# Single transposes between the wide matmuls of a projection, in a fixed order, in place of blocks of four or eight

## The chip, the cores and the metric

The kernel runs on one core of one Trainium2 chip. The core has five engines that work side by side, each through its own list of instructions: TensorE (PE in the profile; its weight loads are listed as PEld) multiplies matrices into PSUM banks, VectorE (DVE) and ScalarE (ACT) do arithmetic on rows, GpSimd (POOL) does slower arithmetic and issues DMAs, SyncE (SP) issues DMAs. The engines wait for one another by semaphores. The metric is the device time of one execution in microseconds, a median over runs.

## The reference

Two layers work on 2048 latent tokens and 256 context tokens of 1024 numbers each. Layer 0 is latent attention beside gated linear attention; layer 1, around which most of the change lies, is a neighbourhood attention with a gate:

```python
h = rms_norm(x, norm_g[i]) * (1 + scale) + shift          # hc likewise from the context
...
q, k, v, z = jnp.split(jnp.dot(h, w_in), 4, axis=-1)      # od_w_in is 1024 x 4096
q, k = rms_norm(sh(q), q_gain), rms_norm(sh(k), k_gain)   # 16 heads of 64
o = neighborhood_attention(q, k, v, k_ctx, v_ctx, rpb)    # window of 8 x 16 on a grid of 32 x 64, and the context
y = jnp.dot(o.reshape(h.shape[0], h.shape[1], C_WIDTH) * jax.nn.silu(z), w_out)
x = x + gate * y
```

Layer 0 has gates of the same form: a projection z times the sigmoid of itself, multiplied onto the attention's output. All is float32.

## The kernel before, in words

**Tiles.** The 256 context and 2048 latent tokens are 18 tiles of 128 tokens (`NT`, two of them context, `NCT`). A projection of a tile is done in cells: one cell is one tile by one block of 512 output columns. The 1024 inputs are eight steps of 128. A float32 product is three products of reduced parts (high by high, high by low, low by high), so that a cell is 8 x 3 = 24 matmuls of 128 x 128 by 512 columns into one PSUM bank. These are the wide matmuls, lines L129 to L131 in `mm3_steps` (L120 to L122 in `mm3`, which other stages use). Their tile is named `gm`.

**Stages.** One after the other on TensorE, with some overlap: layer 0's latent projections, layer 0's gates and the rest of its projections (`even_rest`), layer 0's attention, its output projection, layer 1's queries, keys and half of a gate (`odd_qk`), layer 1's values and the other gates (`odd_vz`), layer 1's attention and output.

**Where transposes stand.** The matmul contracts over partitions, so what comes out with tokens on partitions must be transposed wherever the next product wants it the other way. A transpose is a matmul against the identity, 128 columns.

- `transposed` (L318 to L332): a tile's normalized x, eight transposes into two PSUM banks `px` (L331), once per tile in `odd_qk` and in layer 0. `modulate` scales and shifts them on ScalarE, splits them into high and low parts on VectorE (tiles `hhi`, `hlo`) and stores the result to H from ScalarE's DMA queue. In the later stages `reload` loads H back and splits it (L357).
- `odd_qk`, cell L1117 to L1141, `fin` L1143 to L1182: a finished cell is squared on ScalarE (`osq`), summed on VectorE and raised to a power on GpSimd (`oss`), scaled on VectorE (`onat`, L1139). A gate cell (j = 6) has a tanh on ScalarE and a product on VectorE instead. The cell goes to a list `pend`; `fin` transposes it four times into one bank `tp` (L1147), splits it (`oqh`, `oql`, `okt`) and stores it: queries and keys on SyncE's queue, keys in a second form and the gates on GpSimd's.
- `odd_vz`, cell L1221 to L1243: the cells j = 6 and 7 of latent tiles are gates: tanh, product (`ovz`, L1199), four transposes (L1239), a copy `ozt`, a store on ScalarE's queue.
- `even_rest`, cell L611 to L636: the same for column block 0, with tiles `u` and `zt`; 18 such cells.

**Score maxima.** In `even_rest` and `odd_vz` a second stream of matmuls runs between the projection's: scores of queries against keys, of which VectorE takes row maxima. In `odd_vz` (L1251 to L1300) they are two 256-column matmuls per pair of query tiles (L1273) and one of up to 480 columns per query tile (L1280) into five banks `mx`; GpSimd builds a table of bias and mask for every head (`mtab`, L1258 and L1259).

**What sets the order.** The code of the kernel is traced once; every instruction has a priority by its place in the trace. A planner, which simulates the engines when the kernel is built, then orders each engine's instructions: of those whose inputs it believes ready it takes the first by priority. `issue_after(a)` binds an instruction to come behind `a` on its engine; the rest is free. `weave` draws wide matmuls (three at a time) and score matmuls alternately at a given ratio and binds the wide ones behind earlier score matmuls. `stream` goes through the cells and prepares the next tile when a tile's last cell is done. `pump` draws splits of the next weights (`split_steps`, tiles `wraw` to `w0h` and so on), which ScalarE and VectorE do.

In `odd_qk` the transposes of a cell come into the trace in the middle of a later cell:

```python
for n, _ in enumerate(steps):
    if n == 5 and pend and (len(pend) > 1 or j == 6):
        fin(*pend.pop(0))
    yield
```

with `n` the step of eight. Everywhere else they come right behind what makes their input, and the planner places them by its own times.

Of the kernel before, what the change touches and what calls it, by code (L numbers as in the profile page):

```python
# [17 lines left out]
P = 128  # L18
D = 1024
KD = D // P  # L20
# [4 lines left out]
NCT = CTX // P  # L25
# [63 lines left out]
class Kern:  # L89
    def __init__(self, tc, nc, ins, scr):  # L90
        self.tc, self.nc, self.i, self.scr = tc, nc, ins, scr
        self.n = 0
        self.ahead, self.calls, self.chain = [], 0, None

# [19 lines left out]
    def mm3(self, out, lhs, rhs, ks, start=True, stop=True):  # L114

        lh, ll = lhs
        rh, rl = rhs
        n = len(ks)
        for j, k in enumerate(ks):
            self.nc.tensor.matmul(out, lh(k), rh(k), start=start and j == 0, stop=False)  # L120
            self.nc.tensor.matmul(out, lh(k), rl(k), start=False, stop=False)
            self.nc.tensor.matmul(out, ll(k), rh(k), start=False, stop=stop and j == n - 1)  # L122

    def mm3_steps(self, out, lhs, rhs, ks):
        lh, ll = lhs
        rh, rl = rhs
        n = len(ks)
        for j, k in enumerate(ks):
            self.nc.tensor.matmul(out, lh(k), rh(k), start=j == 0, stop=False)  # L129
            self.nc.tensor.matmul(out, lh(k), rl(k), start=False, stop=False)  # L130
            yield self.nc.tensor.matmul(out, ll(k), rh(k), start=False, stop=j == n - 1)  # L131
# [46 lines left out]
    def stream(self, cells, hT, cell, prep, done=None):  # L178
# [8 lines left out]
        for n, (t, j) in enumerate(cells):  # L187
            yield from cell(t, j)
# [128 lines left out]

    def transposed(self, t, src, pp, tag, xp=None):  # L318

# [9 lines left out]
        ps = [self.tl(pp, [P, 4, P], tag[0], bufs=tag[1]) for _ in range(2)]  # L329
        for k in range(KD):  # L330
            nc.tensor.transpose(ps[k // 4][:, k % 4, :], x[:, k * P : k * P + P], self.ident[:])  # L331
        return x, ps, hi, lo  # L332
# [267 lines left out]
    def even_rest(self, ws, win, hT):  # L600
        nc = self.nc
        self.zaT = self.scr("zaT", (4, P, T), F32)
        with ExitStack() as es:
# [5 lines left out]
            def cell(t, j):  # L609
# [12 lines left out]
                if j == 0:  # L622
                    pt = self.tl(pp, [P, 4, P], "tp", bufs=1)
                    for b in range(4):
                        nc.tensor.transpose(pt[:, b, :], u[:, b * P : b * P + P], self.ident[:])
                    z = self.tl(sp, [P, 4, P], "zt")
                    self.act(z[:], pt[:])
                    nc.gpsimd.dma_start(self.zaT[:, :, t * P : t * P + P].rearrange("j p t -> p j t"), z[:])
                elif j == 1:
                    nc.gpsimd.dma_start(self.Un[t, :, 1056:], u[:])  # L630
                else:
                    nc.gpsimd.dma_start(self.Un[t, :, (j - 2) * 352 : (j - 1) * 352], u[:, :352])

# [1059 lines left out]
```

## Time and profile before

| | us |
|---|---|
| median of 3 runs | 3750.93 |
| lowest and highest of these | 3749.34 and 3751.32 |
| the profiled execution, span | 3751.7 |
| layer 0, latent projections (0 to 552 of the span): TensorE busy | 510.7 |
| `even_rest` (552 to 1092): TensorE busy | 533.3 |
| layer 0's attention (1092 to 1986): TensorE busy | 880.6 |
| layer 0's output projection (1986 to 2189): TensorE busy | 201.3 |
| `odd_qk` (2189 to 2644): TensorE busy | 436.8 |
| `odd_vz` (2644 to 3118): TensorE busy | 462.2 |
| layer 1's attention and output (3118 to the end): TensorE busy | 562.1 |

The span is the profiled execution's own time, from its first instruction to its last. The stage borders are read from where the lines of TensorE change. How the rows shown below are read: in the first part of the page stand each engine's busy time, its share of the span and its number of instructions. A row of a stretch has start and end, length, the busy times of TensorE, its weight loads, VectorE, ScalarE and GpSimd with their instructions in brackets, then the granted TensorE clock (1 is full speed), the busy share of the DMA engines and GB/s. A row of the timeline has start, duration, engine, line, operation, output and inputs, shape; `x4` means that four instructions stand together in it; a bracket at the end names a wait, its length, and what ended it. A row of waits has who waits, what ended it, the total, the number of times and the longest.

### The profile page before, as it was taken

To read this page: it belongs to the slowest core of one execution; us is meant where nothing else is said; L and a number is where in the kernel's file an instruction comes from. 1 tells how busy PE (TensorE), PEld (TensorE's weight loads), DVE (VectorE), ACT (ScalarE), POOL (GpSimd) and SP (SyncE) were. 2 spreads that over 40 slices of the span, in tenths; PEclk is the share of its full clock that TensorE was granted. 3 is DMA by queue.
4 is the path that set the end of the run, shared out by engine and by line. 5 is a ranking of instruction groups with operands and counts; after the bars stand their busy time and mean duration, and the time that the engine had idled before them with its cause. 6 is when DMAs were issued, how large, how long until landed. Compare 5 with 4: busy or idle time off the path is not lost.

```text
span 3751.7 us, 51747 instructions
## 1 busy us (share of the span) xinstructions
PE 3587.1 (96%) x18404; PEld 2772.4 (74%) x18404; DVE 2375.7 (63%) x4860; ACT 1437.8 (38%) x2741; POOL 1206.8 (32%) x1336
## 2 busy tenths in 40 slices
PE   7999989999999999999999999999899999898889
PEld 6988988888886666656657878887688886555567
DVE  4677656888866666696754344455578774666722
ACT  4445541111125555545552134444222224444400
POOL 1434320010111222212202233333444435776643
PEclk9999999999999999999999999999999999999899
DMA  7455453222252231425515545545544448777464
GB/s 254 138 161 162 130 168 96 80 81 80 77 134 66 75 108 57 117 82 149 143 37 180 162 141 155 148 146 166 178 138 147 127 114 225 188 183 201 140 194 131
DMA packets 364371, 512.18 MB, mean 137 GB/s; under 512 B 25825, under 2 KB 243889, under 8 KB 358210
## 3 DMA queue, kind: packets, MB, share of 16 engines
q1 hardware_dynamic: 322642, 425.49, 39.5%
q0 software_dynamic: 19872, 55.92, 4.9%
q10 hardware_dynamic: 21600, 27.46, 2.1%
q8 instruction: 146, 2.39, 0.3%
q14 instruction: 111, 0.91, 0.1%
HBM read 329.38 MB, written 179.37 MB: 136 GB/s over the span
## 4 chain that ended last, share of the span: by engine, by line
PE 78%; DVE 8%; DMA 6%; POOL 4%; ACT 3%; issue 2%; SPq 0%; POOLq 0%; DVEq 0%; ACTq 0%
PE gm L129 9%; PE gm L130 9%; PE gm L131 9%; PE av L905 7%; PE st L963 4%; PE mx L651 4%; PE st L964 3%; PE st L965 3%; PE pj L129 3%; PE pj L130 3%; PE pj L131 3%; POOL oacc L1409 2%; PE o L1403 1%; DMA wraw<-w_od 1%; PE st L1373 1%
## 5 line engine op out<-in xcount | busy, mean ns | idle before, releaser
L954 DVE TENSOR_TENSOR acc<-acc,apt 128x512 f32<-128x512 f32 x512 | 364.6, 737 | 155.3 <-ACT apt L106 152.3
L106 ACT ACTIVATE apt<-st 128x512 f32<-128x512 f32 (+1 forms) x592 | 343.9, 593 | 282.5 <-PE st L965 245.3
L652 DVE TENSOR_REDUCE mm<-mx 128x1 f32<-128x512 f32 (+1 forms) x656 | 389.2, 629 | 82.1 <-PE mx L651 75.1
L905 PE MATMUL av<-apt,av 128*64 128x512 f32 (+1 forms) x1184 | 286.2, 597 | 0.0
L963 PE MATMUL st<-aq,akh 97*128 97x512 f32 (+1 forms) x592 | 254.0, 429 | 5.8 <-ACT apt L106 3.0
L1409 POOL TENSOR_TENSOR oacc<-oacc,opt 128x576 f32<-128x576 f32 (+6 forms) x192 | 221.4, 1178 | 87.0 <-ACT opt L106 85.3
L651 PE MATMUL mx<-mk,mq 96*128 96x512 f32 (+1 forms) x656 | 236.8, 373 | 6.1 <-DMA mq<-QT 4.7
L964 PE MATMUL st<-aq,akh 96*128 96x512 f32 (+1 forms) x592 | 235.1, 397 | 0.0
L965 PE MATMUL st<-aq,akl 96*128 96x512 f32 (+1 forms) x592 | 234.0, 396 | 0.0
L1286 DVE CUSTOM_DVE_ANT_1 mx<-mx,mtab 128x225 f32<-128x225 f32 (+12 forms) x576 | 183.8, 339 | 61.4 <-PE mx L1280 45.9
L106 ACT ACTIVATE u<-gm 128x352 f32<-128x352 f32 (+1 forms) x140 | 68.5, 497 | 369.8 <-PE gm L131 208.8
L905 PEld LDWEIGHTS av<-apt,av 128*64 128x64 f32 x1184 | 81.6, 137 | 155.3 <-issue 154.1
L1531 DVE TENSOR_TENSOR opt<-st,tab 128x64 f32<-128x64 f32 (+10 forms) x576 | 142.5, 314 | 78.7 <-PE st L1374 50.8
L963 PEld LDWEIGHTS st<-aq,akh 97*128 97x128 f32 x592 | 112.4, 190 | 98.9 <-issue 43.7
L1073 POOL TENSOR_TENSOR px<-py,px 128x512 f32<-128x512 f32 x64 | 86.2, 1348 | 231.5 <-DVE py L1072 220.4
L106 ACT ACTIVATE opt<-opt 128x930 f32<-128x930 f32 (+8 forms) x130 | 104.4, 805 | 138.1 <-DVE opt L1531 129.3
L1373 PE MATMUL st<-q,kt 128*128 128x480 f32 (+5 forms) x256 | 104.3, 409 | 47.2 <-DVE opt L1531 42.5
L651 PEld LDWEIGHTS mx<-mk,mq 96*128 96x128 f32 x656 | 121.7, 189 | 17.7 <-issue 5.1
L106 ACT ACTIVATE prh<-pr 128x1024 fp32r<-128x1024 f32 x32 | 33.9, 1058 | 263.4 <-PE pj L130 235.7
L965 PEld LDWEIGHTS st<-aq,akl 96*128 96x128 f32 x592 | 113.5, 192 | 25.5
L964 PEld LDWEIGHTS st<-aq,akh 96*128 96x128 f32 x592 | 114.1, 193 | 18.0
L106 ACT ACTIVATE x<-px,modB,modA 128x128 f32<-128x128 f32 x272 | 99.1, 468 | 57.9 <-DVE onat L1139 27.6
(513 smaller groups left out, 10054.6 us busy)
## 6 DMA issues: line engine op xcount, KB each, us to landing
q<-Q SPq DMA_DIRECT2D x48, 512.0 KB
H<-x ACTq DMA_DIRECT2D x36, 512.0 KB
adaw<-ada_w SPq DMA_DIRECT2D x64, 256.0 KB
x<-H SPq DMA_DIRECT2D x32, 512.0 KB
pr<-RT SPq DMA_DIRECT2D x32, 512.0 KB
wraw<-w_od SPq DMA_DIRECT2D x64, 256.0 KB
K1t<-okt POOLq DMA_DIRECT2D x32, 512.0 KB, 7.7
kt<-K1t SPq DMA_DIRECT2D x32, 512.0 KB
```

The source lines that it names most:

```text
L106: return self.nc.scalar.activation(out, in_, func, **kw)
L129: self.nc.tensor.matmul(out, lh(k), rh(k), start=j == 0, stop=False)
L130: self.nc.tensor.matmul(out, lh(k), rl(k), start=False, stop=False)
L131: yield self.nc.tensor.matmul(out, ll(k), rh(k), start=False, stop=j == n - 1)
L651: mm = nc.tensor.matmul(ps[:, :w], q[:A_QK, (t % 6) * P : (t % 6) * P + P], k[:A_QK, k0 : k0 + w], start=True, stop=True)
L652: nc.vector.tensor_reduce(out=m[:, t, n : n + 1], in_=ps[:, :w], axis=AX.X, op=ALU.max)
L905: nc.tensor.matmul(O[j, nb][i * 64 : i * 64 + 64, :w], V[j, kt // TT][:, kt % TT, i * 64 : i * 64 + 64], pts[i][:, :w], start=n == 0, stop ...
L954: nc.vector.tensor_tensor(out=acc[i][:, :w], in0=a[:, :w], in1=pts[i][:, :w], op=ALU.add)
L963: nc.tensor.matmul(ps[:, :w], kh[: A_QK + 1, i, kq], qh[: A_QK + 1, :w], start=True, stop=False)
L964: nc.tensor.matmul(ps[:, :w], kh[:A_QK, i, kq], ql[:A_QK, :w], start=False, stop=False)
L965: mm = nc.tensor.matmul(ps[:, :w], kl[:A_QK, i, kq], qh[:A_QK, :w], start=False, stop=True)
L1409: self.psum = nc.gpsimd.tensor_tensor(out=a, in0=a, in1=pts[:, :, a0 - r0 : a1 - r0, :], op=ALU.add)
```

## The change

Transposes of the four places above no longer come in blocks. A new list `narrow` holds tasks; a task is a generator of transposes with a due count and a spacing. Every wide matmul of `mm3` and `mm3_steps` now goes through `mm`, which counts it (`wide`), and, if a task is due, emits that task's next transpose bound behind this wide matmul; the next wide matmul is bound behind the transpose (`hold`). The task is then due again three wide matmuls later. So the order of wide matmuls and transposes is as traced; score matmuls and all other engines stay with the planner.

- A tile's x in `odd_qk`: `prep_task`, due 26 wide matmuls after the tile that frees its buffers has ended; `stream` finishes what is left of it before the tile's first cell.
- A projection in `odd_qk`: queued at step 2 of a later cell, at once due, where it was emitted as a block at step 5. What follows the transposes (`split`) is traced behind the last of them.
- Gates of `odd_vz` and `even_rest`: queued at the end of their cell, due nine wide matmuls later.

Transposes still in the list at the end of a stage are emitted in a block (`finish_tasks`). The numbers of instructions on every engine are the same in both kernels: 16410 on TensorE, 4862 on VectorE, 2705 on ScalarE, 1341 on GpSimd, 1151 on SyncE as built.

```diff
         self.ahead, self.calls, self.chain = [], 0, None
+        self.narrow, self.wide, self.hold = [], 0, None
     def pool(self, es, name, bufs=1, space=None, **kw):
...
         return self.chain
-    def mm3(self, out, lhs, rhs, ks, start=True, stop=True):
-
-        lh, ll = lhs
-        rh, rl = rhs
-        n = len(ks)
-        for j, k in enumerate(ks):
-            self.nc.tensor.matmul(out, lh(k), rh(k), start=start and j == 0, stop=False)
-            self.nc.tensor.matmul(out, lh(k), rl(k), start=False, stop=False)
-            self.nc.tensor.matmul(out, ll(k), rh(k), start=False, stop=stop and j == n - 1)
+    def queue(self, gen, wait=0, every=3):
+        task = [self.wide + wait, every, gen]
+        self.narrow.append(task)
+        return task
+    def finish_tasks(self):
+        while self.narrow:
+            self.finish_task(self.narrow[0])
+    def finish_task(self, task):
+        if task in self.narrow:
+            self.narrow.remove(task)
+        for _ in task[2]:
+            pass
+    def mm(self, out, l, r, start, stop):
+        with self.tc.issue_after(self.hold.ins) if self.hold else ExitStack():
+            mm = self.nc.tensor.matmul(out, l, r, start=start, stop=stop)
+        self.hold = None
+        self.wide += 1
+        for task in self.narrow:
+            if task[0] <= self.wide:
+                with self.tc.issue_after(mm.ins):
+                    self.hold = next(task[2], None)
+                if self.hold is None:
+                    self.narrow.remove(task)
+                task[0] = self.wide + task[1]
+                break
+        return mm
+    def mm3(self, *a):
+        for _ in self.mm3_steps(*a):
+            pass
     def mm3_steps(self, out, lhs, rhs, ks):
...
         for j, k in enumerate(ks):
-            self.nc.tensor.matmul(out, lh(k), rh(k), start=j == 0, stop=False)
-            self.nc.tensor.matmul(out, lh(k), rl(k), start=False, stop=False)
-            yield self.nc.tensor.matmul(out, ll(k), rh(k), start=False, stop=j == n - 1)
+            self.mm(out, lh(k), rh(k), j == 0, False)
+            self.mm(out, lh(k), rl(k), False, False)
+            yield self.mm(out, ll(k), rh(k), False, j == n - 1)
+    def transposes(self, ps, parts, src, done):
+        for n, i in enumerate(parts):
+            t = self.nc.tensor.transpose(ps(i), src(i), self.ident[:])
+            if n == len(parts) - 1:
+                done()
+            yield t
     def weave(self, main, side, ratio, lag, head=0):
...
         for n, (t, j) in enumerate(cells):
+            if len(hT[t]) > 2:
+                self.finish_task(hT[t][2])
+                hT[t] = hT[t][:2]
             yield from cell(t, j)
...
         return self.modulate(l, t, *self.transposed(t, src, pp, tag))
+    def prep_task(self, l, t, src, pp, tag, wait):
+        x, hi, lo = self.scaled(t, src)
+        def steps():
+            ps = []
+            for g in range(2):
+                ps.append(self.tl(pp, [P, 4, P], tag[0], bufs=tag[1]))
+                done = (lambda: self.modulate(l, t, x, ps, hi, lo)) if g else lambda: None
+                yield from self.transposes(lambda k: ps[g][:, k, :], range(4), lambda k: x[:, (g * 4 + k) * P : (g * 4 + k + 1) * P], done)
+        return hi, lo, self.queue(steps(), wait)
     def transposed(self, t, src, pp, tag, xp=None):
+        x, hi, lo = self.scaled(t, src, xp)
+        ps = [self.tl(pp, [P, 4, P], tag[0], bufs=tag[1]) for _ in range(2)]
+        for k in range(KD):
+            self.nc.tensor.transpose(ps[k // 4][:, k % 4, :], x[:, k * P : k * P + P], self.ident[:])
+        return x, ps, hi, lo
+    def scaled(self, t, src, xp=None):
         nc, sp = self.nc, self.prp
...
         nc.vector.tensor_scalar(out=x[:], in0=x[:], scalar1=ss[:, 1:2], scalar2=None, op0=ALU.mult)
-        ps = [self.tl(pp, [P, 4, P], tag[0], bufs=tag[1]) for _ in range(2)]
-        for k in range(KD):
-            nc.tensor.transpose(ps[k // 4][:, k % 4, :], x[:, k * P : k * P + P], self.ident[:])
-        return x, ps, hi, lo
+        return x, hi, lo
     def modulate(self, l, t, x, ps, hi, lo):
...
                 if j == 0:
-                    pt = self.tl(pp, [P, 4, P], "tp", bufs=1)
-                    for b in range(4):
-                        nc.tensor.transpose(pt[:, b, :], u[:, b * P : b * P + P], self.ident[:])
-                    z = self.tl(sp, [P, 4, P], "zt")
-                    self.act(z[:], pt[:])
-                    nc.gpsimd.dma_start(self.zaT[:, :, t * P : t * P + P].rearrange("j p t -> p j t"), z[:])
+                    self.queue(turned(t, u), 9)
                 elif j == 1:
                     nc.gpsimd.dma_start(self.Un[t, :, 1056:], u[:])
                 else:
                     nc.gpsimd.dma_start(self.Un[t, :, (j - 2) * 352 : (j - 1) * 352], u[:, :352])
+            def turned(t, u):
+                pt = self.tl(pp, [P, 4, P], "tp", bufs=1)
+                def store():
+                    z = self.tl(sp, [P, 4, P], "zt")
+                    self.act(z[:], pt[:])
+                    nc.gpsimd.dma_start(self.zaT[:, :, t * P : t * P + P].rearrange("j p t -> p j t"), z[:])
+                yield from self.transposes(lambda b: pt[:, b, :], range(4), lambda b: u[:, b * P : b * P + P], store)
             cells = self.cells(list(range(NT))[::-1], (2, 3, 4, 0, 1), lambda t, j: j not in (2, 3) or t < NT - 2)
...
             self.weave(gemms, maxes(), 1.06, 30, 20)
+            self.finish_tasks()
     @staticmethod
...
                 for n, _ in enumerate(steps):
-                    if n == 5 and pend and (len(pend) > 1 or j == 6):
-                        fin(*pend.pop(0))
+                    if n == 2 and pend and (len(pend) > 1 or j == 6):
+                        self.queue(fin(*pend.pop(0)))
                     yield
...
             def fin(t, j, n):
+                ps = self.tl(pp, [P, 4, P], "tp")
+                yield from self.transposes(lambda i: ps[:, i, :], range(4), lambda i: n[:, i * P : i * P + P], lambda: split(t, j, ps))
+            def split(t, j, ps):
                 z = j // 2
-                ps = self.tl(pp, [P, 4, P], "tp")
-                for i in range(4):
-                    nc.tensor.transpose(ps[:, i, :], n[:, i * P : i * P + P], self.ident[:])
                 hi = self.tl(sp, [P, 4, P], "oqh", F32R)
...
             cells += [(t, j) for j in (0, 1, 2, 3, 6) for t in (NT - 2, NT - 1)]
-            for _ in self.stream(cells, hT, cell, lambda t: self.prep(1, t, self.x1, pp, ("px", 2)), done):
+            for _ in self.stream(cells, hT, cell, lambda t: self.prep_task(1, t, self.x1, pp, ("px", 2), 26), done):
                 self.pump()
-            while pend:
-                fin(*pend.pop(0))
+            for p in pend:
+                self.queue(fin(*p))
+            self.finish_tasks()
     def gate(self, out, in_):
...
                 self.gate(n, ps[:])
+                self.queue(turned(t, j, n), 9)
+            def turned(t, j, n):
                 pt = self.tl(pp, [P, 4, P], "tp", bufs=1)
-                for i in range(4):
-                    nc.tensor.transpose(pt[:, i, :], n[:, i * P : i * P + P], self.ident[:])
-                z = self.tl(sp, [P, 4, P], "ozt", bufs=1)
-                self.act(z[:], pt[:])
-                o = (t - NCT) * P
-                nc.scalar.dma_start(self.z1[(j - 6) * 4 : (j - 6) * 4 + 4, :, o : o + P].rearrange("j p t -> p j t"), z[:])
+                def store():
+                    z = self.tl(sp, [P, 4, P], "ozt", bufs=1)
+                    self.act(z[:], pt[:])
+                    o = (t - NCT) * P
+                    nc.scalar.dma_start(self.z1[(j - 6) * 4 : (j - 6) * 4 + 4, :, o : o + P].rearrange("j p t -> p j t"), z[:])
+                yield from self.transposes(lambda i: pt[:, i, :], range(4), lambda i: n[:, i * P : i * P + P], store)
             zq = [[self.tl(mp, [P, 512], f"mz{i}{a}", F32R, bufs=1) for a in range(2)] for i in range(2)]
...
             self.weave(gemms, maxes(), 0.57, 15)
+            self.finish_tasks()
     def odd_attention(self, out, right, left, wout):
```

## Prediction

> **What bounds the kernel.** I read the page's first part, then the table by stage, then the waits by who waited for whom. The rows are, in this order, the engines' busy time, layer 1's query/key stage (2189 to 2644 us of the span) and its value/gate stage (2644 to 3118 us), and what TensorE waited for at transposes in these two (total, times, longest).
>
> ```profile
> PE 3587.1 (96%) x18404; PEld 2772.4 (74%) x18404; DVE 2375.7 (63%) x4860; ACT 1437.8 (38%) x2741; POOL 1206.8 (32%) x1336
> ...
> 2189.00:2644.00 455.00, 436.75 (x2092) 359.69 (x2091) 235.41 (x366) 216.72 (x412) 170.18 (x214) 0.98 0.54 160
> 2644.00:3118.00 474.00, 462.24 (x2229) 384.22 (x2229) 327.98 (x1365) 117.43 (x194) 191.28 (x172) 0.99 0.47 143
> ...
> PE tp L1147 <- DVE onat L1139: 7.2, 3, 4.5
> PE tp L1147 <- ACT oqh L106: 5.4, 1, 5.4
> PE px L331 <- DVE x L328: 3.6, 1, 3.6
> PE tp L1239 <- DVE ovz L1199: 3.2, 2, 2.4
> ```
>
> TensorE is the bound: busy 436.8 of 455 us and 462.2 of 474 us. So the change counts by what it does to TensorE's stream, in two ways: the price of a transpose, and waits. The waits at transposes add up to 7.2 + 5.4 + 3.6 + 3.2 = 19.4 us, and come seven times. That is all that better placing could win; the many other transposes already find their data ready.
>
> **The price of a transpose.** The rows are TensorE's timeline: start, duration, line. Two wide matmuls (512 columns) stand around four, around eight, and around one.
>
> ```profile
> 2311.47 0.39 PE L131 MATMUL gm<-w2h,hlo 128*128 128x512 f32 x1
> 2311.70 0.60 PE L1147 MATMUL tp<-ident,onat 128*128 128x128 f32 x4
> ...
> 2312.37 0.39 PE L130 MATMUL gm<-w2l,hhi 128*128 128x512 f32 x1
> ...
> 2304.18 0.40 PE L129 MATMUL gm<-w1h,hhi 128*128 128x512 f32 x1
> 2304.42 1.03 PE L331 MATMUL px<-ident,x 128*128 128x128 f32 x8
> ...
> 2305.52 0.40 PE L131 MATMUL gm<-w1h,hlo 128*128 128x512 f32 x1
> ...
> 3087.53 0.40 PE L129 MATMUL gm<-w2h,hhi 128*128 128x512 f32 x1
> 3087.76 0.27 PE L1293 MATMUL mx<-ident,mc 128*16 128x128 f32 x1
> ...
> 3088.11 0.39 PE L131 MATMUL gm<-w2h,hlo 128*128 128x512 f32 x1
> ```
>
> Wide matmuls start 0.23 us apart (2311.47 to 2311.70), two steps are 0.46. With four transposes between, the wide matmul after next starts at 0.90: 0.44 for four, 0.11 each. With eight it is 1.34: 0.88, again 0.11. With a single one it is 3088.11 - 3087.53 = 0.58: 0.12. A lone transpose is not cheaper than one in a block; by these rows it costs 0 to 0.015 us more. The built order of the changed kernel has 583 transposes alone or in pairs (112 of x, 471 of projections and gates) where the old one had them mostly in fours and eights. I take 0.006 each, half a step of the printed digits: **+3.5 us** (0 to +9). Numbers of instructions and of DMAs on every engine and queue are unchanged.
>
> The Trainium skill, "TensorE: Matmul & The Clock Gate", sections "Wait — 56ns, not 53.3ns?" and on the architecture, states a start-to-start of 55.6 ns for 128 columns and that the queue pulls weight loads ahead of matmuls in flight. By that a lone transpose would hide its load and cost 0.056: 583 x 0.054 = 31 us won. The lone transpose of the trace, 0.12, does not agree: the next wide matmul's own load stays bare.
>
> **Query/key stage, steady part.** The old order put a projection's four transposes 42 wide matmuls behind the end of its cell; the new one puts the first at 33, the last at 42. The chain behind a cell is square, sum, power, scale:
>
> ```profile
> 2301.01 0.60 ACT L106 ACTIVATE osq<-gm 128x512 f32<-128x512 f32 x1 [0.71 <-PE gm L131]
> ...
> 2304.37 0.69 DVE L1139 TENSOR_TENSOR onat<-gm,oss 128x512 f32<-128x512 f32 x1 [2.05 <-POOL oss L202]
> ...
> 2218.88 0.80 PE L129 MATMUL gm<-w0h,hhi 128*128 128x512 f32 x1
> ...
> 2229.20 1.06 ACT L106 ACTIVATE hlo<-x 128x1024 fp32r<-128x1024 f32 x1 [8.94 <-DMA x<-x]
> 2231.31 0.75 DVE L328 TENSOR_SCALAR x<-x,ssx 128x1024 f32<-128x1024 f32 x1 [7.10 <-POOL ssx L202]
> ```
>
> From 2301.01 to 2305.06 it takes 4.1 us against 33 x 0.23 = 7.6 us: covered, 0. The eight of x wait 26 wide matmuls by the code, but the planner put ten of the next cell before them: 36, that is 8.3 us, covered too. Not at the stage's start: tile 2's first matmul is at 2218.88, tile 3's x is ready at 2231.31 + 0.75 = 2232.06 because its load waits for the store of the x before it. The old order came to it after 58 wide matmuls, the new after 36: 36 x 0.23 + 0.5 for the transposes + some 2.5 for the slow clock there makes 2230.2: **+2 us** (0 to 4).
>
> **End of the query/key stage.** Here ScalarE and VectorE take weight splits in order with the chains, and the weights' loads are late. The last row is a stretch of 10 us; the third number from its end, 0.67, is the granted clock.
>
> ```profile
> 2620.18 1.26 ACT L106 ACTIVATE w0h<-wraw 128x512 fp32r<-128x512 f32 x2 [2.37 <-DMA wraw<-w_od]
> ...
> 2622.09 0.68 DVE L1139 TENSOR_TENSOR onat<-gm,oss 128x512 f32<-128x512 f32 x1
> ...
> 2622.92 0.63 PE L1147 MATMUL tp<-ident,onat 128*128 128x128 f32 x4 [1.80 <-DVE onat L1139]
> ...
> 2634.98 1.09 PE L1147 MATMUL tp<-ident,onat 128*128 128x128 f32 x4 [4.54 <-DVE onat L1139]
> ...
> 2640.53 0.63 ACT L106 ACTIVATE w1h<-wraw 128x512 fp32r<-128x512 f32 x1 [4.02 <-DMA wraw<-w_od]
> ...
> 2642.83 1.12 PE L1147 MATMUL tp<-ident,onat 128*128 128x128 f32 x4 [5.42 <-ACT oqh L106]
> ...
> 2630.00:2640.00 10.00, 2.64 (x10) 1.44 (x9) 4.38 (x7) 4.51 (x7) 2.06 (x2) 0.67 0.92 312
> ```
>
> These waits are for weights, whose time TensorE does not set. A transpose eight wide matmuls earlier in a fixed order waits 1.8 us more there; the later wait shrinks by as much. What remains is at the end: in the new order the two last gates' products stand on ScalarE and VectorE behind the sixth and seventh piece of the weights (the sixth is split at 2640.53), where the old order had them behind the fourth and fifth. From 2640.53 a split, a table load, tanh and product follow, some 3.5 us, then the seventh piece and the second gate, some 3 more: the last four transposes come near 2647, not 2642.83: **+4 us** (-4 to +8; below nothing if the new order's loads come earlier).
>
> **Start of the value/gate stage.** The old order ran both first cells (48 wide matmuls) and then transposed; the new one has the first transpose of cell 1's gate nine wide matmuls into cell 2.
>
> ```profile
> 2646.68 0.76 POOL L1151 DMA_DIRECT2D z<-oqh  x1
> ...
> 2657.24 1.03 DVE L1248 MEMSET mz<- 64x512 f32 x2 [6.54 <-DMA z<-oqh]
> ...
> 2658.37 1.21 DVE L1199 SCALAR_TENSOR_TENSOR ovz<-ovz,gm 128x512 f32<-128x512 f32 x2
> ...
> 2659.05 0.66 PE L1239 MATMUL tp<-ident,ovz 128*128 128x128 f32 x4 [2.42 <-DVE ovz L1199]
> ```
>
> VectorE's gate product stands behind a memset that waits for the last z store, so the data comes at 2659 whatever TensorE does, 16 us after the stage's last transposes. The 15 wide matmuls that would have covered the wait are now behind it: 15 x 0.23 = 3.5 us, and a wait of some 6 us brings the half clock that 0.67 above shows, some 2 more: **+5.5 us** (+2 to +9). The same page of the Trainium skill ("What's actually happening") has the clock fall after an idle window of 3.4 us; the 0.67 beside waits of 4.54 and 5.42 agrees.
>
> **The other gates.** In this stage the first transpose stands 9 wide and mostly 8 score matmuls (mx) behind its cell's end. Rows of one tile boundary: the cell's last wide matmul, what score matmuls take, and the gate; then an undisturbed boundary.
>
> ```profile
> 2805.92 0.40 PE L1273 MATMUL mx<-mk,mz 128*128 128x256 f32 x2
> 2806.16 0.33 PE L1280 MATMUL mx<-mk,mz 128*128 128x360 f32 x1
> 2806.32 0.40 PE L130 MATMUL gm<-w3l,hhi 128*128 128x512 f32 x1
> 2806.55 0.39 PE L131 MATMUL gm<-w3h,hlo 128*128 128x512 f32 x1
> ...
> 2807.59 3.72 POOL L1259 TENSOR_TENSOR mtab<-mtab,maskq 128x1798 f32<-128x1798 f32 x1
> ...
> 2808.12 4.26 DVE L357 TENSOR_TENSOR hlo<-x,hhi 128x1024 fp32r<-128x1024 f32 x1
> 2812.31 0.68 DVE L1199 SCALAR_TENSOR_TENSOR ovz<-ovz,gm 128x512 f32<-128x512 f32 x1
> ...
> 2778.78 1.22 DVE L357 TENSOR_TENSOR hlo<-x,hhi 128x1024 fp32r<-128x1024 f32 x1
> ```
>
> Three score matmuls take 0.40 us (2805.92 to 2806.32), eight 1.1. So the transpose is due 10 x 0.23 + 1.1 = 3.4 us after 2806.55, and its data comes at 2812.99, 6.4 after: 3 us of wait, which the old order covered with 22 or more wide matmuls. VectorE's split took 4.26 instead of 1.22 because GpSimd's table add ran until 2811.31. (The Trainium skill, "SBUF — State Buffer", on the shared port pair, calls this an exclusive lock held for the whole instruction; 2811.31 plus 1.07 is when the split ended, which agrees.) Without the add the data comes some 3 us earlier, just in time. With three such boundaries (3 + 2 + 2) and nothing at the others, as the planner's own fill suggests: **+7 us** (+1 to +20; the upper end if the bunched score matmuls run out of their five banks at the 30 gates). Layer 0's 18 gates have no table adds beside them and more cover: 0 (0 to +2).
>
> **The sum.** 3.5 + 2 + 4 + 5.5 + 7 = +22 us. The profiled span is 3751.7 us, 0.8 above the median of 3750.93 of the runs; against the median: **3773 us**, +0.6%. A difference under 0.2% (7.5 us) can't be told from none here.
>
> **Rivals.**
> - Waits stay covered, only the price counts: 3751 + 3 = 3754, no change. For it: the planner moved score and next-cell matmuls into the gaps it saw. Against: it did not see late weights, the z store or GpSimd's hold on VectorE. 0.15.
> - Faster: the fixed spacing takes the old waits away. If of the 19.4 us the 12.6 at projections went and no new wait came, 3751 - 12.6 + 3.5 = 3742. Against: these waits are for weights and ScalarE. It decides if the last transposes of the stage start before 2638 in its time. 0.08.
> - Lone transposes hide their loads (the page's rule): 3751 - 31 = 3720 without waits, near 3740 with them. Against: the 0.12. 0.04.
> - Banks run out at the gates: 30 x 1 us more, 3803. For it: 8 score matmuls need 6 banks of 5. Against: VectorE often waits for TensorE there. 0.08.
> - My forecast: 0.65, its own range 3759 to 3797.
>
> Faster 0.12 (0.08 + 0.04), same 0.15, slower 0.73 (0.65 + 0.08). The range 3750 to 3797 leaves out the faster cases and most of the full banks.
>
> **What would show it.** Lone transposes between wide matmuls at 0.11 to 0.12 us. A wait over 4 us at the first gate transpose of the value/gate stage, and three of 2 to 3 us at later tile boundaries behind the gate product. No waits in the steady query/key part, whose 22 to 24 us per tile grow by under 0.3. The prediction is wrong if lone transposes cost under 0.10, if the end of the query/key stage moves by over 8 us either way, or if waits for score banks appear.

## The result and the profile after

The changed kernel takes 3776.76 us (median of 4 runs, 3773.30 to 3784.41) against 3750.14 us (4 runs, 3748.91 to 3751.32): 1.0082 of the time before, interval 1.0070 to 1.0094. The forecast was 3773 us. The profiled execution spans 3775.0 us, 23.3 more than the one before.

The table by stage of the changed kernel, the query/key stage and the value/gate stage, cut behind their last transpose and last wide matmul:

```profile
2189.00:2656.50 467.50, 442.46 (x2091) 346.82 (x2090) 233.15 (x366) 218.39 (x412) 176.69 (x214) 0.98 0.52 155
2656.50:3143.50 487.00, 464.78 (x2233) 380.67 (x2232) 321.89 (x1364) 117.55 (x194) 191.64 (x173) 0.99 0.45 140
```

And what TensorE waited for in the two (total, times, longest):

```profile
PE tp L163 <- DVE onat L1264: 9.5, 1, 9.5
PE tp L163 <- DVE onat L1202: 6.9, 5, 4.1
PE px L163 <- DVE x L387: 5.6, 2, 3.0
...
PE tp L163 <- DVE ovz L1264: 11.9, 10, 6.8
PE mx L1364 <- DVE mc L1362: 4.7, 5, 1.8
PE mx L1351 <- DVE mm L1346: 2.6, 2, 1.5
PE mx L1351 <- DVE mm L1357: 2.6, 1, 2.6
```

The stages last 467.5 and 487.0 us where they lasted 455 and 474. TensorE has the same instructions; its busy time rose by 5.7 and 2.5 us, the rest is idle time. The waits at transposes are now 9.5 + 6.9 + 5.6 + 11.9 = 33.9 us, 19.4 before. The last two rows are score matmuls that wait for a bank which VectorE has not yet read: 5.2 us in three waits, 1.3 us in two (0.8 and 0.5) in the kernel before.

Waits do not add up to time, since a wait can take the place of a later one. So I counted TensorE's wide matmuls (`gm`) in each trace, 6784 in both kernels and in the same number per stage, and took the time from one count to another. The stretches are named by what they hold; the counts are in brackets. The column "same order" is the run only_er below, whose layer 1 is instruction for instruction that of the kernel before: how it differs from "before" shows what one execution differs from another, up to 3.6 us in a stretch.

| stretch (wide matmuls) | before | same order | after | after - before |
|---|---|---|---|---|
| layer 0, up to its gates (to 1488) | 557.4 | - | 554.9 | -2.5 |
| layer 0's gates, start (to 1608) | 40.40 | - | 44.48 | +4.1 |
| layer 0's gates, rest (to 3504) | 500.43 | - | 500.32 | -0.1 |
| attention, output projection (to 3552) | 1098.58 | 1096.74 | 1097.17 | -1.4 |
| query/key, start (to 3744) | 56.46 | 54.48 | 61.69 | +5.2 |
| query/key, steady (to 5088) | 347.47 | 347.49 | 351.82 | +4.4 |
| query/key, end (to 5232) | 52.01 | 52.88 | 54.85 | +2.8 |
| value/gate, start (to 5424) | 61.48 | 57.84 | 63.10 | +1.6 |
| value/gate, tile boundaries (to 6744) | 395.39 | 393.20 | 406.62 | +11.2 |
| layer 1's attention and output (to TensorE's end) | 633.49 | 631.17 | 631.42 | -2.1 |

**The lone transpose.** TensorE's timeline in the steady query/key part: wide matmuls with a transpose of x and one of a projection among them.

```profile
2410.51 0.39 PE L134 MATMUL gm<-w1l,hhi 128*128 128x512 f32 x1
2410.74 0.27 PE L163 MATMUL px<-ident,x 128*128 128x128 f32 x1
2410.77 0.47 PE L134 MATMUL gm<-w1h,hlo 128*128 128x512 f32 x1
2411.08 0.39 PE L134 MATMUL gm<-w1h,hhi 128*128 128x512 f32 x1
2411.31 0.27 PE L163 MATMUL tp<-ident,onat 128*128 128x128 f32 x1
2411.34 0.48 PE L134 MATMUL gm<-w1l,hhi 128*128 128x512 f32 x1
```

From 2410.51 to 2411.08 are two wide steps and one transpose: 0.57 - 0.46 = 0.11 us. The next wide matmul starts 0.03 us behind the transpose, but then takes 0.31 to the next start instead of 0.23. A lone transpose costs what one in a block does, to a hundredth. The hundredth is there: between the 3792nd and the 4944th wide matmul (12 tiles, 288 transposes) it is 299.9 against 296.0 us; three places where TensorE waited make 1.2 of these 3.9 (by the starts before and after the wait), which leaves 0.009 per transpose.

**The start of the query/key stage.** The third tile's x: VectorE's scaling, then TensorE.

```profile
2231.08 0.75 DVE L387 TENSOR_SCALAR x<-x,ssx 128x1024 f32<-128x1024 f32 x1 [0.97 <-POOL ssx L240]
...
2228.95 0.40 PE L134 MATMUL gm<-w2h,hhi 128*128 128x512 f32 x1
2231.97 0.30 PE L163 MATMUL px<-ident,x 128*128 128x128 f32 x1 [2.63 <-DVE x L387]
...
2233.20 0.78 PE L134 MATMUL gm<-w1h,hlo 128*128 128x512 f32 x1
2233.78 0.63 PE L134 MATMUL gm<-w1h,hhi 128*128 128x512 f32 x1
2234.20 0.63 PE L134 MATMUL gm<-w1l,hhi 128*128 128x512 f32 x1
```

x is ready at 2231.83, TensorE came to it at 2229.2 and waited 2.63 us; then wide matmuls start 0.42 us apart instead of 0.23 (0.58 in place of 0.31 behind a transpose): the half clock.

**The end of the query/key stage.** ScalarE's timeline, then VectorE's clearing at the next stage's start, then TensorE there.

```profile
2643.59 0.60 ACT L107 ACTIVATE onat<-gm 128x512 f32<-128x512 f32 x1
2652.79 0.63 ACT L107 ACTIVATE w1h<-wraw 128x512 fp32r<-128x512 f32 x1 [7.95 <-DMA wraw<-w_od]
2654.39 0.64 ACT L107 ACTIVATE onat<-gm 128x512 f32<-128x512 f32 x1
...
2670.66 1.02 DVE L1319 MEMSET mz<- 64x512 f32 x2 [7.42 <-DMA K1t<-okt]
2671.79 0.62 DVE L1264 SCALAR_TENSOR_TENSOR ovz<-ovz,gm 128x512 f32<-128x512 f32 x1
...
2672.47 0.47 PE L163 MATMUL tp<-ident,ovz 128*128 128x128 f32 x1 [6.83 <-DVE ovz L1264]
```

A stretch behind that wait and one behind the largest loss at a tile boundary, which comes next (third number from the end: the granted clock):

```profile
2672.40:2675.80 3.40, 3.33 (x10) 2.54 (x11) 0.01 (x1) 0.00 (x0) 2.17 (x1) 0.50 1.00 387
2829.80:2833.20 3.40, 3.40 (x11) 2.51 (x11) 1.88 (x9) 0.90 (x2) 0.00 (x0) 0.50 0.11 42
```

The second gate's tanh (`onat`) stands behind a weight piece that waited 7.95 us for its load. The next stage's first gate waits 6.83 us, because VectorE's product stands behind a clearing that waits for a store of keys; then 3.4 us at a granted clock of 0.50.

**A tile boundary of the value/gate stage.** GpSimd, VectorE and TensorE at the largest loss, 5.6 us:

```profile
2822.43 3.69 POOL L1330 TENSOR_TENSOR mtab<-mtab,maskq 128x1798 f32<-128x1798 f32 x1
...
2822.97 4.23 DVE L413 TENSOR_TENSOR hlo<-x,hhi 128x1024 fp32r<-128x1024 f32 x1
2828.04 0.67 DVE L1264 SCALAR_TENSOR_TENSOR ovz<-ovz,gm 128x512 f32<-128x512 f32 x1
...
2827.63 1.04 PE L1351 MATMUL mx<-mk,mz 128*128 128x360 f32 x2 [2.55 <-DVE mm L1357]
2828.77 0.33 PE L163 MATMUL tp<-ident,ovz 128*128 128x128 f32 x1
```

The split takes 4.23 us under GpSimd's table add (1.23 is the middle value of the stage's 16 splits), gate and score maxima come behind it. The planner has put score matmuls in a row ahead of the transpose, so the wait shows at a score matmul that needs a bank (2.55 us) and not at the transpose. Again 3.4 us of half clock follow. The second largest loss, 2.8 us at the boundary around 2858 us, has no half clock behind it (granted 1.00 from 2855 to 2868 us).

**Layer 0's gates.** The start of that stage:

```profile
574.11 0.49 PE L713 MATMUL mx<-mk,mq 96*128 96x512 f32 x1 [0.81 <-DVE mm L714]
575.58 0.38 PE L713 MATMUL mx<-mk,mq 96*128 96x256 f32 x1 [0.97 <-DVE mm L714]
576.17 1.25 PE L713 MATMUL mx<-mk,mq 96*128 96x512 f32 x2 [0.21 <-DVE mm L714]
577.46 0.45 PE L163 MATMUL tp<-ident,u 128*128 128x128 f32 x1
577.56 0.78 PE L134 MATMUL gm<-WUh,hhi 128*128 128x512 f32 x1
578.13 0.63 PE L134 MATMUL gm<-WUl,hhi 128*128 128x512 f32 x1
```

Four score matmuls stand in a row ahead of the first gate's transpose and take turns with VectorE's maxima; wide matmuls then run at half clock.

### The profile page after: what moved, and what is told of

It is laid out like the page before. It is cut to its first block, busy times and chain, and to the rows that moved or that the text cites. A ratio compares the mean times of both kernels' runs of the same rounds, so it can differ in the third digit from the quotient of the medians.

```text
span 3775.0 us, 51760 instructions
## 1 busy us (share of the span) xinstructions
PE 3591.2 (95%) x18404; PEld 2746.2 (73%) x18404; DVE 2366.7 (63%) x4860; ACT 1441.1 (38%) x2741; POOL 1215.5 (32%) x1336
## 5 line engine op out<-in xcount | busy, mean ns | idle before, releaser
L1357 DVE CUSTOM_DVE_ANT_1 mx<-mx,mtab 128x225 f32<-128x225 f32 (+15 forms) x576 | 182.1, 341 | 74.2 <-PE mx L1351 56.1
L107 ACT ACTIVATE prh<-pr 128x1024 fp32r<-128x1024 f32 x32 | 33.9, 1058 | 260.9 <-PE pj L134 233.2
```

The source lines that it names most:

```text
L107: return self.nc.scalar.activation(out, in_, func, **kw)
L1357: nc.vector.tensor_tensor_reduce(out=s, in0=s, in1=tb[:, ri : ri + rn, ci : ci + cn], scale=1.0, scalar=-3e38, op0=ALU.add, op1=ALU.max, a ...
```

## The experiments

Each run was compared with the kernel before on the same chip. Each part of the change can be taken back alone; with all four taken back the order of every engine is that of the kernel before. In the diffs `-` is the changed kernel.

### One part of the change alone

```diff
 # x in blocks
-self.prep_task(1, t, self.x1, pp, ("px", 2), 26)
+self.prep(1, t, self.x1, pp, ("px", 2))
 # projections in blocks
-if n == 2 and pend and (len(pend) > 1 or j == 6):
-    self.queue(fin(*pend.pop(0)))
+if n == 5 and pend and (len(pend) > 1 or j == 6):
+    for _ in fin(*pend.pop(0)): pass
 # gates of the value/gate stage in blocks (those of layer 0 likewise)
-self.queue(turned(t, j, n), 9)
+for _ in turned(t, j, n): pass
```

Four kernels, each with three of these four taken back. Only x:

> The kernel before with one part of the change: the eight transposes of a tile's x in the query/key stage are emitted singly; projections and gates stay in blocks of four. The change as a whole costs 26.6 us (3776.8 against 3750.1). Theory (waits at a few places; the lone transpose itself costs next to nothing): the wide matmul that was 0.3 us ahead before the third tile is 4.9 us behind after it, so this part costs +5 us, all of it at that stage's start. Rival 1 (a price per lone transpose, the same everywhere: 26.6 us / 583 = 0.046 each): 112 x 0.046 = +5 us too, but spread evenly, 0.37 per tile. Rival 2 (the parts only cost together): 0 to +2 us.

Only the projections:

> The kernel before with one part of the change: the projections' transposes of the query/key stage are emitted singly, queued at step 2 of a later cell; x and the gates stay in blocks. Theory (waits): in the changed kernel's steady part a tile takes 0.2 to 0.3 us more, 12 tiles some 3 us, and at the stage's end some 3 us are lost in front of the last gates: +6 us (3 to 9). Rival 1 (price per lone transpose, 0.046): 272 x 0.046 = +12.5 us, the dearest part of the four. Rival 2 (only together): 0 to +2 us.

Only the value/gate stage's gates:

> The kernel before with one part of the change: the gates' transposes of the value/gate stage are emitted singly from nine wide matmuls behind their cell. Theory (waits): the wait in front of the first gate (5 to 7 us, of which some is given back) and two or more tile boundaries at which the score maxima and the gate stand behind a split that the table add holds up (5.6 and 2.8 us in the changed kernel): +10 us (7 to 15), the dearest part. Rival 1 (price, 0.046): 120 x 0.046 = +5.5 us, evenly spread. Rival 2 (only together, as the end of the query/key stage came 12 us later): +2 us or less.

Only layer 0's gates:

> The kernel before with one part of the change: the gates' transposes of layer 0 are emitted singly. Theory (waits): 3.5 us are lost at the stage's start, where four score matmuls come in a row and the clock halves, and some of it is given back where the next stage begins: +2 us (0 to 4). Rival 1 (price, 0.046): 72 x 0.046 = +3.3 us, evenly over the stage. Rival 2 (only together): 0.

| part alone | of the time before | interval | in us of 3744.3 |
|---|---|---|---|
| x | 1.0018 | 1.0009 to 1.0027 | +7 |
| projections | 1.0022 | 1.0013 to 1.0031 | +8 |
| value/gate stage's gates | 1.0041 | 1.0027 to 1.0054 | +15 |
| layer 0's gates | 1.0002 | 0.9993 to 1.0010 | +1 |

The sum is 1.0083, the whole change 1.0082. Expected were 5, 6, 10 (7 to 15) and 2 us. The 120 transposes of the value/gate stage cost twice what 272 of projections cost, so a price per transpose is out. But the sum hides that x and the projections share a loss: each alone costs the stage's start 6 to 9 us (63.04 and 62.21 us for the stretch, 54.48 to 56.46 before), both together 5 to 7. For the projections that was not expected: I had put their loss into the steady part and the end, which take 1.9 and 1 to 2 us more. With projections alone the wait at the start is at a projection, behind x on VectorE:

```profile
PE tp L163 <- DVE onat L1203: 4.4, 1, 4.4
```

With x alone it is at a projection as well (5.22 us, the same tile `onat`), not at x.

Layer 0's gates alone take 5.1 us more at their stage's start (45.53 us for the stretch, 40.40 before); the time of the whole run does not show it. Executions of one and the same order differ by up to 5 us in the long stretch of layer 0's attention (1094.53 to 1099.75 us in the runs that leave layer 0 as it was), so a loss of this size can't be told from that by the time alone.

### Blocks at the same places

```diff
-with self.tc.issue_after(mm.ins):
-    self.hold = next(task[2], None)
...
-task[0] = self.wide + task[1]
+self.narrow.remove(task); self.hold = mm
+while True:
+    with self.tc.issue_after(self.hold.ins):
+        t = next(task[2], None)
+    if t is None: break
+    self.hold = t
```

> The changed kernel, but a task that is due emits all its transposes in one block behind that wide matmul: the place of the first transpose stays, the others move up to it. Theory (the place and its waits): stays near the changed kernel, 1.007 to 1.009 of the kernel before; the steady query/key part wins the 0.2 to 0.3 us per tile that lone transposes cost, 3 to 4 us in all, and blocks of the not yet finished data lose none. Rival (lone transposes are what costs): back to 1.002 or less.

1.0038 (1.0024 to 1.0052): less than half of the loss is left, and my expectation was wrong. By the medians 16 us are won; the profiled execution, which is the longest of this kernel's six (3756 to 3773 us), shows 11 to 12 of them in two stretches: the steady query/key part takes 347.36 us, as before the change (351.82 with lone ones), and the stage's end 47.58 (54.85). Start of that stage (61.02), start of the next (64.39) and tile boundaries (406.80) stay lost. At the end it is ScalarE's order:

```profile
2640.45 0.60 ACT L107 ACTIVATE onat<-gm 128x512 f32<-128x512 f32 x1
...
2648.23 0.63 ACT L107 ACTIVATE w1h<-wraw 128x512 fp32r<-128x512 f32 x1 [4.18 <-DMA wraw<-w_od]
2648.77 0.58 ACT L107 ACTIVATE onat<-gm 128x512 f32<-128x512 f32 x1
```

With blocks four and six pieces of w1 stand ahead of the two tanh, with lone transposes six and seven, in the kernel before four and five (counted on ScalarE's timeline). A group of four that is stretched over ten wide matmuls has its split that much later, and the planner gives ScalarE weight pieces in the meantime; that this is why was not tested by itself. So lone transposes do cost: 4 us in the steady part, and 7 at the end, where another engine's order moved with them.

### Later places

```diff
-self.queue(turned(t, j, n), 9)
+self.queue(turned(t, j, n), 27)
```

The value/gate stage's gates alone, as in the third run, but due 27 wide matmuls behind their cell:

> The kernel before with only the value/gate stage's gates emitted singly, but due 27 wide matmuls behind their cell in place of 9. Theory (waits): with 27 x 0.23 = 6.2 us and the score matmuls' 3 us more the first gate and the tile boundaries are covered; of the +15 us (1.0041) of the run with 9 at most 3 us are left: 1.000 to 1.001. Rival 1 (price of lone transposes): stays at 1.003 or more. Rival 2 (fixed order binds score matmuls, which run out of banks in any place): stays at 1.003 or more, with the waits at score matmuls.

1.0010 (1.0001 to 1.0018), against 1.0041 with 9: three quarters of this part's loss is the place. The tile boundaries take 397.56 us (407.70 with 9). What TensorE waited for in that stage, first with 9, then with 27:

```profile
PE tp L163 <- DVE ovz L1267: 11.5, 10, 6.4
PE mx L1367 <- DVE mc L1365: 4.2, 5, 1.8
...
PE mx L1354 <- DVE mm L1360: 2.6, 1, 2.6
```

```profile
PE mx L1367 <- DVE mc L1365: 9.6, 11, 3.0
...
PE gm L134 <- DVE ovz L1267: 2.5, 1, 2.5
```

No transpose waits for `ovz` any more. Instead, a wide matmul waits 2.5 us for it once (its PSUM bank is still to be read), and the waits for a head's row maxima (`mc`) are twice those with 9 (7.2 us in the kernel before). Then the whole change with later places, x at 48 in place of 26 and both stages' gates at 27:

> The changed kernel, all transposes single, with later places: x due 48 wide matmuls after the tile before (26 in the changed kernel), gates in both stages 27 behind their cell (9). Theory (waits): the start of the query/key stage loses its 5 us, the value/gate stage some 11 of 15, layer 0's gates nothing; what stays is the projections' part with the end of the query/key stage and 4 us of price: 1.002 to 1.0035. Rival (price of lone transposes above all): 1.006 or more.

1.0048 (1.0036 to 1.0061): a miss to the high side. Layer 0's start is back at 40.26 us and the tile boundaries at 395.31, both as before. But the start of the query/key stage still takes 61.38, since a projection now waits where x waited, and the steady part 354.12, more than with 26. For x, 48 is no better place. A later place for the projections was not tried, so what of the rest is their place stays open.

### What makes the gates late

GpSimd's table adds in four pieces each (the second add, by columns, likewise in the same loop):

```diff
-nc.gpsimd.tensor_tensor(out=tb[:], in0=tb[:], in1=mk[:, :NR].unsqueeze(2).to_broadcast([P, NR, NC]), op=ALU.add)
+cut = [NR * i // 4 for i in range(5)]
+for r0, r1 in zip(cut, cut[1:]):
+    s = tb[:, r0:r1, :]
+    nc.gpsimd.tensor_tensor(out=s, in0=s, in1=mk[:, r0:r1].unsqueeze(2).to_broadcast([P, r1 - r0, NC]), op=ALU.add)
```

> The changed kernel with each of GpSimd's two table adds (3.2 and 3.7 us) cut into four pieces of rows, the same work. Theory (VectorE's split of a reloaded tile stands still for a whole instruction of GpSimd): splits that took 4.2 us take 1.2 to 2.3, the waits at 2825 and 2858 us of the changed kernel (5.6 and 2.8 us with the slow clock) go: 6 to 9 us less than the changed kernel, 1.006. Rival 1 (both engines share access piece by piece): splits still take some 4 us and the time stays at 1.008. Rival 2 (the waits are for score banks because VectorE has too much work): the splits are faster, the time stays at 1.008.

1.0070 (1.0058 to 1.0082), which the intervals do not tell from the changed kernel's 1.0082; 1.006 was expected. At 2823 and 2853 us the splits took 1.95 and 1.39 us, and of the waits at both places 0.4 us or less is left each time. At another boundary a worse one came:

```profile
3030.95 6.05 DVE L413 TENSOR_TENSOR hlo<-x,hhi 128x1024 fp32r<-128x1024 f32 x1
3036.93 0.67 DVE L1264 SCALAR_TENSOR_TENSOR ovz<-ovz,gm 128x512 f32<-128x512 f32 x1
...
3028.24 3.64 POOL L1332 TENSOR_TENSOR mtab<-mtab,maskq 128x434 f32<-128x434 f32 x4
3031.85 4.07 POOL L1333 TENSOR_TENSOR mtab<-mtab,maskq 128x434 f32<-128x434 f32 x4
```

The split began under the fourth of GpSimd's eight pieces and stood until the last of them (they follow each other without a pause from 3028.24 to 3035.92). TensorE waited 4.78 us there, so the stretch takes 406.04 us, as much as before the cut. That the add holds VectorE is shown; that shorter adds let it in holds only sometimes: at the first two places the split ended 1.08 us after the first piece that it met, here after the fifth.

The clearing on GpSimd:

```diff
-nc.vector.memset(z[64 - i * 64 : 128 - i * 64].bitcast(F32), 0.0)
+nc.gpsimd.memset(z[64 - i * 64 : 128 - i * 64].bitcast(F32), 0.0)
```

> The changed kernel with the clearing of the score operands (memset mz) on GpSimd in place of VectorE, so that the gate product no longer stands behind a clearing that waits for a z store. Theory: the wait of 6.8 us at the first gate transpose of the value/gate stage falls below 1.5 us; up to 5 of it had been given back within the stage, so the time falls by 1.5 to 6 us, to 1.0065 to 1.008. Rival (the wait is the gates' own chain, which comes late from the stage before): the wait stays above 4 us, 1.008.

1.0077 (1.0063 to 1.0091), no difference from the changed kernel that the intervals tell. The wait fell from 6.8 to 5.0 us only; it was 5.6 in the run with the cut adds, which leaves the clearing where it was. With the clearing elsewhere, VectorE's next instruction in line waits for the same store:

```profile
2671.46 0.22 DVE L1332 MEMSET mm<- 128x80 f32 x2 [12.44 <-DMA K1t<-okt]
2671.59 0.63 DVE L1264 SCALAR_TENSOR_TENSOR ovz<-ovz,gm 128x512 f32<-128x512 f32 x1
```

So it is not this clearing but the first use of the new stage's buffers, which must wait until the last keys of the stage before are stored.

The last weights behind the tanh: the last 16 steps of the query/key stage draw no weight pieces, and those drawn in the next stage are bound behind the last tanh (`behind`).

```diff
-self.act(hi[:, s, c], w[:])
+with self.tc.issue_after(self.behind.ins) if self.behind else ExitStack():
+    self.act(hi[:, s, c], w[:])
```

> The changed kernel; the last weights of the query/key stage (eight splits on ScalarE of w1, needed by the fifth cell of the next stage) are bound behind the tanh of the last gate, where six and seven of them stood ahead of the two tanh. Theory (the last gates wait behind weight pieces whose loads are late): the wait of 9.7 us in front of the last block of four falls below 3 us, the following one at the first gate of the next stage stays; 5 to 8 us won at the end of the stage, 1.006 to 1.007. Rival 1 (given back: the first gate of the value/gate stage waits for a store of that stage anyway): that wait grows by as much, 1.008. Rival 2 (the late splits hold up the fifth cell): a wait at w1, 1.008 or more.

1.0083 (1.0069 to 1.0096): nothing won. The wait in front of the last gate fell from 9.5 to 2.3 us, as expected, and the end of the stage takes 47.65 us instead of 54.85. The next stage's start gave 4.0 back (67.07 for 63.10): the wait at that stage's first gate went from 6.8 to 11.7 us. This is the first rival, though with less than the whole 7.2 us. ScalarE:

```profile
2664.51 0.63 ACT L107 ACTIVATE w1h<-wraw 128x512 fp32r<-128x512 f32 x1 [8.04 <-DMA wraw<-w_od]
2666.59 0.63 ACT L107 ACTIVATE w1h<-wraw 128x512 fp32r<-128x512 f32 x1 [1.45 <-DMA wraw<-w_od]
2667.13 0.58 ACT L107 ACTIVATE ovz<-gm 128x512 f32<-128x512 f32 x1
```

The same late weight pieces now stand ahead of the next gate's tanh (`ovz`). Of 7.2 us won at the end 3 are left, which one execution cannot tell from chance.

### Two versions meant to be better

The kernel before with both mends:

> The kernel before (blocks), with the splits of w1 bound behind the last tanh and the clearing of the score operands on GpSimd. Theory: of the kernel before's 12 us of waits at the stage's last transposes (2.2, 4.5 and 5.4) and 2.4 at the next stage's first gate, 5 to 10 go: 0.9975 to 0.9985. Rival (what is won comes back as a wait for w1, or the loads set the time): 0.9995 to 1.0005.

0.9992 (0.9983 to 1.0001). The end of the query/key stage takes 44.05 us (52.01 and 52.88 without), the start of the next 64.03 (61.48 and 57.84): of 8 to 9 us won, 2.5 to 6 come back. 3 us by the median, which the interval does not tell from none.

The fixed order in blocks, at the later places, with both mends:

> All together with the changed kernel's fixed order: blocks in place of lone transposes, at the later places (48 and 27), w1 behind the tanh, the clearing on GpSimd. Theory (only place and waits matter, and some 4 us of price): the fixed order then costs nothing and the two mends win what they win in blocks: 0.997 to 1.000. Rival (a fixed order costs in itself, as the planner's own places fill gaps that nobody can name ahead): 1.002 or more.

1.0011 (1.0002 to 1.0020), above what I expected. The steady part (347.68) costs nothing, but the start of the query/key stage (57.78) and the tile boundaries (399.22) stay above the planner's own order (54.39 and 392.66 in the run above). Against that run, which has the same two mends, the fixed order costs 0.0019, 7 us; the rival's 1.002 was meant against the kernel before, where 1.0011 lies between it and the expectation. No version beat the kernel before by more than can be measured.

## Why the prediction was right, and where not

The time, its sign and its range held: 3776.8 for 3773. The places of the waits were mostly right, the sizes less so. The terms of the sum, by the stretches above:

- **Price of lone transposes: +3.5 forecast.** +4.4 measured in the steady query/key part, 1.2 of it waits. Per transpose that is 0.009 where 0.006 was forecast; for all 583 an estimate by this figure is 5 us, but layer 0's rest, with most of that stage's 72 lone transposes, shows none (500.32 against 500.43 us). That it is the singleness was shown by blocks at the same places, which take it to 0. That a lone transpose hides its load did not happen: 0.11 alone and in blocks, and not the 0.056 for 128 columns that the Trainium skill gives (page "TensorE: Matmul & The Clock Gate", section "Wait — 56ns, not 53.3ns?").
- **Start of the query/key stage: +2 forecast, +5.2 measured,** +7.2 against the other execution with the same order. Right place and right cause: x ready at 2231.83 (2232.06 forecast), TensorE there at 2229.2 (2230.2 forecast). The term that was too small is the half clock that follows the wait; I had counted the slow clock of the time before it and not the new one. And the step "projections: covered, 0" does not hold at the start: a projection there waits behind x on VectorE, which alone would cost as much.
- **End of the query/key stage: +4 forecast, +2.8.** The gates stood behind the sixth and seventh weight piece as forecast. I had taken it for an effect of the earlier place; the run with blocks at the same places shows that it is one of the singleness.
- **Start of the value/gate stage: +5.5 forecast, +1.6** against the profiled execution before, +5.3 against the other with the same order. The wait was 6.83 us (6 forecast) with 3.4 us of half clock. In the changed kernel the clearing waits for a store of keys, where the trace of the kernel before names the last z store, and moving the clearing away did not help.
- **Other tile boundaries: +7 forecast, +11.2.** The mechanism, a split of over 4 us under a table add with the gate behind it, was right at one boundary. The size was not: I had three waits of 2 to 3 us behind the gate product and no half clock; two places took 5.6 us (half clock included) and 2.8 us, and small waits at others the rest. Behind the gate product itself stand only 5.1 us in nine waits. That the largest wait fell on bunched score matmuls is what the rival with the banks described, at two or three boundaries and not at 30. Waits for score banks were one of the prediction's own signs of being wrong, and they came: 5.2 us in three waits.
- **Layer 0's gates: 0 (0 to +2) forecast, +4.1.** Wrong. I had looked for table adds, which are not there, and at the gates in the stage's middle (500.32 us, as before). The loss is at the stage's start, where the planner bunched four score matmuls ahead of the first transpose. With gates due at 27 it is gone (40.26).

The forecast of 22 and the 23.3 between the profiled spans agree better than the terms do, which are off by 1 to 4 us, to both sides. That is in part luck: the six stretches of the terms add up to 29.3 us, and 6.1 are taken off by the other four, of which three hold nothing that was changed. The medians give 26.6. The steady part's tiles grew by 0.31 us on average, where under 0.3 was named as the sign. The rival of the old waits vanishing is out: the 19.4 us became 33.9.

## What to carry to other kernels

A fixed place for an instruction must be covered at the worst cell, not at the average one: the gates lost little at most boundaries and most of their 15 us at a few. A wait of 2.6 us cost nearly two more at two places (3.4 us at half clock), so waits are to be counted with that part where it comes; it does not come behind every wait of this length. And what is moved on one engine moves the order of the others: here six weight pieces instead of four ahead of a tanh on ScalarE made 7 us at the end of a stage, and of what putting that right won there, more than half came back at the next wait for the same loads.

## What was not expected of the hardware

- Waits of 2.63 and 2.55 us of TensorE were followed by the half clock (granted 0.50 over 3.4 us from 2829.8). The Trainium skill, page "TensorE: Matmul & The Clock Gate", section "What's actually happening", gives an idle window of about 3.4 us; here less sufficed. The length of a wait does not decide it: 1.92 us at 2696.87 in the kernel before were followed by the half clock, 2.97 us at 2955.95 in the run with gates due at 27 were not (first and second row; the third number from the end is the granted clock). What decides was not tested.

```profile
2698.30:2701.70 3.40, 3.40 (x10) 2.71 (x9) 1.97 (x13) 0.00 (x0) 1.77 (x4) 0.50 0.68 242
2956.00:2959.40 3.40, 3.40 (x20) 2.84 (x21) 2.67 (x15) 0.27 (x1) 2.35 (x4) 1.00 0.98 365
```

- VectorE's split took 6.05 us while the last five of eight short adds of GpSimd followed each other, longer than the 4.23 us under one long add: cutting an instruction into pieces does not by itself let the other engine in.
